# A transformer trunk on one core: the modulation steps moved off the keys and doubled in the later MLP, and the merge ordered by branches

## The chip, the cores and the metric

The kernel runs on one core of a Trainium2 chip. The metric is the device time of one execution in microseconds. Three runs of the kernel before gave 1308.4, 1308.9 and 1310.21, so its median is 1308.9 us.

## What is computed

The reference is a backbone of two layers over 512 tokens of 1024 channels, 256 of context and 256 latent ones on a grid. Cut to what matters:

```
for l in range(2):
    mod_lat = silu(c) @ w_ada[l] + b_ada[l]          # 6 x 1024: shift, scale, gate, twice
    mod_ctx = silu(c_ctx) @ w_ada[l] + b_ada[l]
    h = rms_norm(x) * (1 + sc1) + sh1                # context and latent, each with its own
    p = h @ w_in                                     # gate logits | c_q | c_kv | k_r | na q, k, v
    mq, mk, mv = from rms_norm(c_q) @ w_uq, rms_norm(c_kv) @ w_ukv, with rope
    y_mla = dense attention of 8 heads;  y_na = neighbourhood attention of 8 heads
    y = sigmoid(gates_a) * (y_mla @ w_mla_o) + sigmoid(gates_b) * (y_na @ w_na_o)
    x = x + gt1 * (y @ w_out)
    h2 = rms_norm(x) * (1 + sc2) + sh2
    x = x + gt2 * (relu(h2 @ w_ff1)**2 @ w_ff2)
```

In the last layer the context's queries, merge and MLP are left out, since only the latent stream is returned.

## The kernel before

Channels lie on the partitions and tokens along the free dimension. Every large product is made of three fp32r matmuls (`mm3`, L101 to L103): weights and data are split into a high and a low part, and high by high, high by low and low by high are added in PSUM. A weight tile of 128x1024 goes this way: SP issues its load into a ring of five raw buffers (`wraw`, L118), ScalarE writes the high part (`wsplit`, L129, `whi`), VectorE writes what is left (L130, `wlo`). There are three pairs of `whi` and `wlo`. The raw ring is shared by all weights and by the rows of the modulation, and SP issues all of them in the order of the program.

`proj_a` (L134) walks over output tiles in chunks of 128 channels. A chunk is 24 matmuls; after it come the evacuation, and one call of `step()` (L150).

`step` (L171) advances the side work, a generator that `ada_side` (L235) makes: the modulation, a product of one or two vectors with `w_ada`, done on VectorE. One part is 1024 of the 6x1024 outputs. A step of a part loads one block of 128 rows of `w_ada` (512 KB) and multiplies and adds it for each vector z (L250 for the first block, L254 afterwards). A step with both vectors is called one of two columns here, a step with one vector one of one column. Behind eight such steps come, per vector, a step that transposes and reduces in VectorE (L265, L266), and one that adds over the partitions on PE (L272) and writes `modT` (L276). The pieces are issued behind the last `wlo` of the moment (`issue_after(lead())`).

Three sides matter. The first makes the gate of the attention of layer 0: eleven steps of two columns, with four accumulators of 512 columns. Before, four of them are taken in the evacuation of the keys (`evac` of `w_ukv`, L743 and L744), and six in the chunks of the gates. What is left is done at `step(99)` behind the gates. The last side is made in the MLP of layer 0: seven parts of what layer 0's MLP and layer 1 need, the first three of two columns (33 steps), the last four of one column (40 steps). Before, each chunk of the MLP takes one step, each ff2 block but the last is closed by `step(4)` (L1200), and two steps are left for the end of the layer.

The MLP is run as ff1(0), ff1(1), ff2(0), ff1(2), ff2(1), ff1(3), ff2(2), ff2(3), each of eight chunks; "third block" below means ff1(2), and "second ff2 block" ff2(1).

The merge (L1031 to L1056) walks over pairs of output tiles. A pair has a weight tile of each branch (a for MLA, b for the neighbourhood attention). Before, for each of its two chunks j both branches are multiplied, then VectorE forms (gate + 1) * product for both (L1048), POOL adds the two (L1052, `m`; VectorE in the last pair), ScalarE takes the high part (L1053, `h`) and POOL what is left (L1054).

The products of each engine's queue are laid out by the scheduler of the framework from this program; within a queue, an engine keeps that order.

Of the kernel before, what the change touches and what calls it, by code (L numbers as in the profile page):

```python
# [45 lines left out]
def trunk(ctx: ExitStack, tc, t):  # L46
# [76 lines left out]

    split = []

    def wsplit(src, k, n):
# [6 lines left out]
    def proj_a(w, k0, kc, f0, nf, moves, cols, evac, bank=None, hook=None):  # L133
# [4 lines left out]
        for f in range(0, nf, per):  # L138
            raw = wraw(w, k0, kc, (f0 + f) * 128, per * 128)
            h, lo = wsplit(raw, kc, per * 128)  # L140
            for j in range(per):
                fs = slice(j * 128, (j + 1) * 128)
                o = (ps(bank[(f + j) % len(bank)]) if bank else psx())[:, :N]
                for k in range(kc):
                    if hook:
                        hook(f + j, k)
                    mm3(o, h[:, k, fs], lo[:, k, fs], mh(k)[:, cols], ml(k)[:, cols], k == 0, k == kc - 1)
                evac(f + j, o)
                flush()
                step()  # L150

# [312 lines left out]
    for l in range(DEPTH):  # L464
# [267 lines left out]
        for hf in range(2):  # L732
            def evac(tk, o):
# [7 lines left out]
                if hf == 1 and tk % 2:  # L741
                    k_stat(tk - 1)
                if tk % 2:  # L743
                    step()  # L744

# [286 lines left out]
        for f in range(0, 8, 2):  # L1032
# [3 lines left out]
            wab = [wsplit(wraw(w_, 0, 4, f * 128, 256), 4, 256) for w_ in (wa, wb)]  # L1036
            for j in range(2):
                zs = [None, None]
                fs = slice(j * 128, (j + 1) * 128)
                g2 = g2f[:, :, j]  # L1040
                for b in (0, 1):
                    (h, lo), (yh, yl) = wab[b], ys[b]
                    o = psx()[:, :TQ]
                    for k in range(4):
                        mm3(o, h[:, k, fs], lo[:, k, fs], yh(k), yl(k), k == 0, k == 3)
                    zs[b] = o
                for b in range(2):
                    nc.vector.scalar_tensor_tensor(out=g2[:, b], in0=g2[:, b], scalar=1.0, in1=zs[b],  # L1048
                                                   op0=ALU.add, op1=ALU.mult)
                eng = nc.vector if f + j >= 6 else nc.gpsimd  # L1050
                m = sp.tile([128, TT], F32, tag="tmp", name="m", bufs=NTMP)
                eng.tensor_tensor(out=m[:, :TQ], in0=g2[:, 0], in1=g2[:, 1], op=ALU.add)  # L1052
                nc.scalar.activation(out=gh[:, f + j, :], in_=m[:, :TQ], func=AF.Copy)  # L1053
# [132 lines left out]
        def ff2(g, a):  # L1186
# [12 lines left out]
            proj_a(t["w_ff2"][l], g * 8, 8, 0, 8, (lambda k: a[0][:, k], lambda k: a[1][:, k]), loc, res_add(GT2))  # L1199
            step(4)  # L1200

# [51 lines left out]
        flush()  # L1253
        step(99)
        pre_ctx = po_ctx

# [54 lines left out]
```

## Time and profile before

| | |
|---|---|
| median of three runs | 1308.9 us |
| the profiled execution | 1308.73 us, span 1306.9 us |
| mean granted clock of PE | 0.994 |
| PE busy | 1272.0 us (97%) |
| VectorE (DVE) busy | 907.8 us (69%) |
| ScalarE (ACT) busy | 582.3 us (45%) |
| POOL busy | 262.3 us (20%) |
| moved by DMA | 208.01 MB, mean 159 GB/s |

The profile is one execution on the chip. A view called a timeline gives instructions with their start and duration, and in brackets how long the engine was idle before and what it then waited for. A window gives busy times of all engines in a stretch, with the clock that TensorE was granted (1.00 is the upper of its two levels, 2.4 GHz; 0.50 the lower, 1.2 GHz). Matmuls are pipelined, so a duration in a timeline is longer than the distance from one start to the next. Where times of one stretch are named, they are microseconds from the start of the span: the keys lie at 97 to 125, the gates at 125 to 158, the attention of layer 0 behind them to 379, its merge at 379 to 426, its MLP at 478 to 826, the start of layer 1 at 826, and the merge of layer 1 at 1063 to 1090.

### The profile page before, as it was taken

What the parts mean: (1) busy time and instruction counts of PE and PEld (TensorE: products, weight loads), DVE (VectorE), ACT (ScalarE), POOL (GpSimd) and SP (SyncE); (2) the same over time, 40 slices, a digit from 0 to 9 for tenths busy, and PEclk for the clock granted to TensorE, in tenths of its full rate; (3) what the DMA queues carried; (4) which work ended last, traced back from release to release, by engine and by line L of the source; (5) the groups of instructions that cost most, each with busy time, mean ns of one, the idle gap of its engine ahead of it and who ended that gap; (6) DMA issues with size and microseconds to landing.
All of it is one profiled execution on the core that took longest, in us unless ns stands there. A gap on an engine that the chain in (4) does not pass through costs nothing.

```text
span 1306.9 us, 20364 instructions
## 1 busy us (share of the span) xinstructions
PE 1272.0 (97%) x7831; PEld 1093.3 (84%) x7831; DVE 907.8 (69%) x1547; ACT 582.3 (45%) x1054; POOL 262.3 (20%) x258
## 2 busy tenths in 40 slices
PE   7998999999999999999999999899999999999997
PEld 5697888986787898888888888899889779999896
DVE  4559687688985579899675675766763967665553
ACT  4455277445523344422322312366664645554452
POOL 0317402411004003210201200019132111121011
PEclk9998999999999999999999999899999999999999
DMA  9855600364486326566566574387214657646652
GB/s 292 291 110 161 209 29 22 100 193 64 110 308 202 99 64 197 163 204 200 167 197 209 170 226 141 115 172 213 74 44 119 129 179 206 169 160 192 193 186 89
DMA packets 241857, 208.01 MB, mean 159 GB/s; under 512 B 24464, under 2 KB 220816, under 8 KB 241376
## 3 DMA queue, kind: packets, MB, share of 16 engines
q1 hardware_dynamic: 231728, 190.16, 50.6%
q10 hardware_dynamic: 9520, 16.29, 3.5%
q8 instruction: 61, 1.00, 0.3%
q0 software_dynamic: 512, 0.27, 0.1%
q14 instruction: 36, 0.29, 0.1%
HBM read 195.15 MB, written 11.53 MB: 158 GB/s over the span
## 4 chain that ended last, share of the span: by engine, by line
PE 55%; DVE 2%; POOL 2%; issue 2%; ACT 1%; DMA 0%; POOLq 0%; ACTq 0%; DVEq 0%
PE psB L101 7%; PE psB L103 7%; PE psB L102 7%; PE psA L101 6%; PE psA L103 6%; PE psA L102 6%; PE psC L103 4%; PE psC L101 4%; PE psC L102 4%; DVE wlo L130 1%; PE psC L872 1%; PE psD L892 1%; ACT whi L129 1%; PE psB L926 1%; PE psD L101 0%
## 5 line engine op out<-in xcount | busy, mean ns | idle before, releaser
L130 DVE TENSOR_TENSOR wlo<-raw,whi 128x1024 fp32r<-128x1024 f32 (+3 forms) x252 | 310.6, 1234 | 189.8 <-ACT whi L129 188.6
L129 ACT ACTIVATE whi<-raw 128x1024 fp32r<-128x1024 f32 (+3 forms) x252 | 260.5, 1035 | 351.3 <-PE psB L102 116.7
L254 DVE SCALAR_TENSOR_TENSOR ada<-raw,silu,ada 128x1024 f32<-128x1024 f32 (+1 forms) x126 | 156.3, 1272 | 0.2
L102 PE MATMUL psA<-wlo,h 128*128 128x256 f32 (+2 forms) x408 | 120.9, 296 | 2.4 <-DVE wlo L130 2.4
L101 PE MATMUL psA<-whi,h 128*128 128x256 f32 (+2 forms) x408 | 121.0, 297 | 1.1 <-ACT h L344 1.1
L103 PE MATMUL psA<-whi,h 128*128 128x256 f32 (+2 forms) x408 | 120.8, 296 | 0.0
L101 PE MATMUL psB<-h,whi 128*128 128x256 f32 (+1 forms) x272 | 91.8, 338 | 0.1
L102 PE MATMUL psB<-h,whi 128*128 128x256 f32 (+1 forms) x272 | 91.8, 338 | 0.0
L103 PE MATMUL psB<-h,wlo 128*128 128x256 f32 (+1 forms) x272 | 91.6, 337 | 0.0
L101 PE MATMUL psA<-h,whi 128*128 128x512 f32 (+1 forms) x248 | 87.6, 354 | 1.1 <-ACT h L344 1.0
L102 PE MATMUL psA<-h,whi 128*128 128x512 f32 (+1 forms) x248 | 87.3, 352 | 0.2 <-DVE h L346 0.2
L103 PE MATMUL psA<-h,wlo 128*128 128x512 f32 (+1 forms) x248 | 87.1, 351 | 0.0
L102 PEld LDWEIGHTS psA<-wlo,h 128*128 128x128 f32 x408 | 78.3, 192 | 4.7 <-DVE wlo L130 2.6
L101 PEld LDWEIGHTS psA<-whi,h 128*128 128x128 f32 x408 | 78.3, 192 | 3.3 <-ACT h L344 1.6
L103 PEld LDWEIGHTS psA<-whi,h 128*128 128x128 f32 x408 | 78.3, 192 | 2.3 <-issue 0.4
L1165 POOL TENSOR_TENSOR h<-s,h 128x512 fp32r<-128x512 f32 (+1 forms) x32 | 38.0, 1190 | 168.5 <-ACT h L1164 151.1
L1165 POOL TENSOR_TENSOR fl<-s,fa 128x512 fp32r<-128x512 f32 (+1 forms) x32 | 35.3, 1104 | 164.8 <-ACT fa L1164 164.8
L101 PE MATMUL psB<-G,whi 128*128 128x512 f32 (+2 forms) x192 | 66.8, 348 | 0.0
L103 PE MATMUL psB<-G,wlo 128*128 128x512 f32 (+2 forms) x192 | 66.3, 345 | 0.3 <-DVE wlo L130 0.3
L102 PE MATMUL psB<-G,whi 128*128 128x512 f32 (+2 forms) x192 | 66.5, 346 | 0.0
L101 PE MATMUL psC<-G,whi 128*128 128x258 f32 (+2 forms) x200 | 62.6, 313 | 0.0
L103 PE MATMUL psC<-G,wlo 128*128 128x258 f32 (+2 forms) x200 | 62.5, 312 | 0.0
(388 smaller groups left out, 3333.0 us busy)
## 6 DMA issues: line engine op xcount, KB each, us to landing
raw<-in_w_ff_dram SPq DMA_DIRECT2D x128, 512.0 KB, 4.3
raw<-in_w_ada_dram SPq DMA_DIRECT2D x80, 512.0 KB, 3.7
raw<-in_w_in_dram SPq DMA_DIRECT2D x62, 512.0 KB, 4.6
raw<-in_w_out_dram SPq DMA_DIRECT2D x16, 512.0 KB, 4.6
spare<-in_w_ada_dram SPq DMA_DIRECT2D x12, 512.0 KB, 8.9
xT_d<-xT SPq DMA_DIRECT2D x2, 2048.0 KB, 13.1
bias<-in_rpb_dram SPq DMA_DIRECT2D x64, 64.0 KB, 7.1
g_d<-g ACTq DMA_DIRECT2D x16, 256.0 KB, 3.9
```

Of the source, the lines that this page charges most:

```text
L101: nc.tensor.matmul(out, sh, mh, start=first, stop=False)
L102: nc.tensor.matmul(out, sh, ml, start=False, stop=False)
L103: nc.tensor.matmul(out, sl, mh, start=False, stop=last)
L129: nc.scalar.activation(out=hi, in_=src, func=AF.Copy)
L130: split[:] = [nc.vector.tensor_tensor(out=lo, in0=src, in1=hi.bitcast(F32), op=ALU.subtract).ins]
L254: nc.vector.scalar_tensor_tensor(out=a, in0=raw[:, c:c + w], scalar=sc, in1=a, op0=ALU.mult, op1=ALU.add)
L872: nc.tensor.transpose(o[:, kt * 256 + i * 128:kt * 256 + (i + 1) * 128], pt[:, (kp * 2 + kt) * 128:(kp * 2 + kt + 1) * 128], perm if K == ...
L892: mm = nc.tensor.matmul(yo[z * 64:(z + 1) * 64, oc], vsel(kt, 2 * hp + z), tr[kt // 2][:, kt % 2, :], start=kt == nkt - 1, stop=kt == 0, t ...
L926: mm = nc.tensor.matmul(os[z], q_[zs, cs], k_[zs, :K], start=n == 0, stop=n == 2)
L1165: nc.gpsimd.tensor_tensor(out=al[:, f, :], in0=s[:, :TQ], in1=ah[:, f, :].bitcast(F32), op=ALU.subtract)
```

## The change

Four edits. No step is taken in the keys any more; the gates still take six, so five are left to `step(99)` behind them. `step(4)` at the end of an ff2 block is replaced by a pace: `proj_a` takes `pace[0]` steps after each chunk, which is 1 until the end of ff2(0) and 2 from there. With two a chunk the side's 73 steps end in ff2(2), none is left for ff2(3) or the layer's end. The merge runs both chunks of branch a, then both of branch b, and forms each (gate + 1) * product right behind its product; the additions, `h` and the rest come behind all four.

```
--- before.py
+++ after.py
@@ -122,6 +122,7 @@
         return raw
 
     split = []
+    pace = [1]
 
     def wsplit(src, k, n):
         hi, lo = hl_tile()
@@ -147,7 +148,7 @@
                     mm3(o, h[:, k, fs], lo[:, k, fs], mh(k)[:, cols], ml(k)[:, cols], k == 0, k == kc - 1)
                 evac(f + j, o)
                 flush()
-                step()
+                step(pace[0])
 
     def proj_tail(w, k0, fs, moves, halves, evac, hook):
 
@@ -740,8 +741,6 @@
                 head_ss(krr[:, tk, hs], dst, 4, NOPE, rs)
                 if hf == 1 and tk % 2:
                     k_stat(tk - 1)
-                if tk % 2:
-                    step()
 
             proj_b(loader(t["w_ukv"][l], 0, hf * 512, 512, 2, 1), 1, lambda k: ch[:, 6 + k], lambda k: cl[:, 6 + k],
                    [0, 1, 2, 3], 512, evac)
@@ -1034,22 +1033,21 @@
                 nc.scalar.dma_start(out=xT, in_=xT_d[:, :, c_q])
             g2f = g2s[f // 2]
             wab = [wsplit(wraw(w_, 0, 4, f * 128, 256), 4, 256) for w_ in (wa, wb)]
-            for j in range(2):
-                zs = [None, None]
-                fs = slice(j * 128, (j + 1) * 128)
-                g2 = g2f[:, :, j]
-                for b in (0, 1):
-                    (h, lo), (yh, yl) = wab[b], ys[b]
+            zs = {}
+            for b in (0, 1):
+                (h, lo), (yh, yl) = wab[b], ys[b]
+                for j in range(2):
+                    fs = slice(j * 128, (j + 1) * 128)
                     o = psx()[:, :TQ]
                     for k in range(4):
                         mm3(o, h[:, k, fs], lo[:, k, fs], yh(k), yl(k), k == 0, k == 3)
-                    zs[b] = o
-                for b in range(2):
-                    nc.vector.scalar_tensor_tensor(out=g2[:, b], in0=g2[:, b], scalar=1.0, in1=zs[b],
+                    zs[b, j] = o
+                    nc.vector.scalar_tensor_tensor(out=g2f[:, b, j], in0=g2f[:, b, j], scalar=1.0, in1=o,
                                                    op0=ALU.add, op1=ALU.mult)
+            for j in range(2):
                 eng = nc.vector if f + j >= 6 else nc.gpsimd
                 m = sp.tile([128, TT], F32, tag="tmp", name="m", bufs=NTMP)
-                eng.tensor_tensor(out=m[:, :TQ], in0=g2[:, 0], in1=g2[:, 1], op=ALU.add)
+                eng.tensor_tensor(out=m[:, :TQ], in0=g2f[:, 0, j], in1=g2f[:, 1, j], op=ALU.add)
                 nc.scalar.activation(out=gh[:, f + j, :], in_=m[:, :TQ], func=AF.Copy)
                 eng.tensor_tensor(out=gl[:, f + j, :], in0=m[:, :TQ], in1=gh[:, f + j, :].bitcast(F32),
                                   op=ALU.subtract)
@@ -1197,7 +1195,7 @@
                 nxt.extend((*nh, acc, norm_1))
                 return
             proj_a(t["w_ff2"][l], g * 8, 8, 0, 8, (lambda k: a[0][:, k], lambda k: a[1][:, k]), loc, res_add(GT2))
-            step(4)
+            pace[0] = 2
 
         if last:
 
@@ -1252,6 +1250,7 @@
         second(3, prev)
         flush()
         step(99)
+        pace[0] = 1
         pre_ctx = po_ctx
 
     po_ctx.close()
```

Line numbers of the kernel after differ by one or two from those before (L250 is L251, L1163 is L1161).

On VectorE in the keys, ahead of the first copy of a key product (L738 before, L739 after), there stood

```order
L250 TENSOR_SCALAR ada<-raw,silu 128x512 x4
L254 SCALAR_TENSOR_TENSOR ada<-raw,silu,ada 128x512 x4
L605 TENSOR_REDUCE qrs<-sq 128x2 x2
L130 TENSOR_TENSOR wlo<-raw,whi 128x1024
L254 SCALAR_TENSOR_TENSOR ada<-raw,silu,ada 128x512 x6
L605 TENSOR_REDUCE qrs<-sq 128x2
L254 SCALAR_TENSOR_TENSOR ada<-raw,silu,ada 128x512 x2
L605 TENSOR_REDUCE qrs<-sq 128x2
L130 TENSOR_TENSOR wlo<-raw,whi 128x1024
L738 COPY mqk<-psB 128x4x64 x2
```

and now there stands

```order
L131 TENSOR_TENSOR wlo<-raw,whi 128x1024
L606 TENSOR_REDUCE qrs<-sq 128x3
L606 TENSOR_REDUCE qrs<-sq 128x2 x2
L131 TENSOR_TENSOR wlo<-raw,whi 128x1024
L606 TENSOR_REDUCE qrs<-sq 128x2
L131 TENSOR_TENSOR wlo<-raw,whi 128x1024
L606 TENSOR_REDUCE qrs<-sq 128x2
L739 COPY mqk<-psB 128x4x64 x2
L251 TENSOR_SCALAR ada<-raw,silu 128x512 x2
```

The sixteen pieces of the modulation ahead of the copy are gone; the first L251 comes behind it. (`qrs` are the sums of squares of the queries.)

On VectorE at the end of the third ff1 block there stood (`s` is the square of the rectified product, L1163 before and L1161 after)

```order
L1163 TENSOR_TENSOR s<-r 128x512
L265 STREAM_TRANSPOSE ada<-ada 128x512 x2
L266 TENSOR_REDUCE red<-ada 128x16 x2
L250 TENSOR_SCALAR ada<-raw,silu 128x1024
L130 TENSOR_TENSOR wlo<-raw,whi 128x1024
L1163 TENSOR_TENSOR s<-r 128x512
L265 STREAM_TRANSPOSE ada<-ada 128x512 x2
L266 TENSOR_REDUCE red<-ada 128x16 x2
L254 SCALAR_TENSOR_TENSOR ada<-raw,silu,ada 128x1024
L276 TENSOR_TENSOR modT_99<-psC,pT 32x16 x4
L130 TENSOR_TENSOR wlo<-raw,whi 128x1024
L1163 TENSOR_TENSOR s<-r 128x512
```

and now

```order
L131 TENSOR_TENSOR wlo<-raw,whi 128x1024
L1161 TENSOR_TENSOR s<-r 128x512
L266 STREAM_TRANSPOSE ada<-ada 128x512 x2
L267 TENSOR_REDUCE red<-ada 128x16 x2
L266 STREAM_TRANSPOSE ada<-ada 128x512 x2
L267 TENSOR_REDUCE red<-ada 128x16 x2
L1161 TENSOR_TENSOR s<-r 128x512
L277 TENSOR_TENSOR modT_99<-psC,pT 32x16 x4
L251 TENSOR_SCALAR ada<-raw,silu 128x1024
L255 SCALAR_TENSOR_TENSOR ada<-raw,silu,ada 128x1024 x4
L1161 TENSOR_TENSOR s<-r 128x512
L131 TENSOR_TENSOR wlo<-raw,whi 128x1024
```

Between the last `wlo` of the third block and the first of the second ff2 block there are now both columns' transposes and reduces, `modT`, and five pieces of the next part. On SP, the loads from the third block's last ones on were, before,

```order
L118 DMA raw<-in_w_ff_dram 128x8x128 x4
L118 DMA raw<-in_w_ada_dram 128x1024
L118 DMA raw<-in_w_ff_dram 128x8x128
L118 DMA raw<-in_w_ada_dram 128x1024
L118 DMA raw<-in_w_ff_dram 128x8x128
```

and are

```order
L118 DMA raw<-in_w_ff_dram 128x8x128 x2
L118 DMA raw<-in_w_ada_dram 128x1024
L118 DMA raw<-in_w_ff_dram 128x8x128
L118 DMA raw<-in_w_ada_dram 128x1024 x2
L118 DMA raw<-in_w_ff_dram 128x8x128
L118 DMA raw<-in_w_ada_dram 128x1024 x2
L118 DMA raw<-in_w_ff_dram 128x8x128
```

Two rows of the modulation stand between two weights, where one did. The last row is the first weight of the second ff2 block.

On VectorE at the boundary of the layers (`h` is the normed input of layer 1, the `wlo` of 576 columns the third weight tile of its first product) there stood

```order
L340 SCALAR_TENSOR_TENSOR u<-xT,A_1_101,psD 128x256
L346 SCALAR_TENSOR_TENSOR h<-u,modT_99,h 128x256
L265 STREAM_TRANSPOSE ada<-ada 128x512
L346 SCALAR_TENSOR_TENSOR h<-u,modT_99,h 128x256
L266 TENSOR_REDUCE red<-ada 128x16
L265 STREAM_TRANSPOSE ada<-ada 128x512
L130 TENSOR_TENSOR wlo<-raw,whi 128x576
L266 TENSOR_REDUCE red<-ada 128x16
L276 TENSOR_TENSOR modT_99<-psC,pT 32x8 x4
L322 TENSOR_SCALAR ms<-psC 128x2
```

and now

```order
L347 SCALAR_TENSOR_TENSOR h<-u,modT_99,h 128x256
L341 SCALAR_TENSOR_TENSOR u<-xT,A_1_101,psD 128x256
L347 SCALAR_TENSOR_TENSOR h<-u,modT_99,h 128x256
L131 TENSOR_TENSOR wlo<-raw,whi 128x576
L347 SCALAR_TENSOR_TENSOR h<-u,modT_99,h 128x256
L323 TENSOR_SCALAR ms<-psC 128x2
L341 SCALAR_TENSOR_TENSOR u<-xT,A_1_101,psC 128x256 x3
```

The two transposes, two reduces and `modT` are gone from between `h` and the first weights and the sum of squares.

## Rows read from the trace of the kernel before

**Rows 1.** The page's first part, of the whole span: busy time, share of the span and instructions of each engine.
```profile
PE 1272.0 (97%) x7831; PEld 1093.3 (84%) x7831; DVE 907.8 (69%) x1547; ACT 582.3 (45%) x1054; POOL 262.3 (20%) x258
```

**Rows 2.** The waits of PE over the whole span: the product that waited (its PSUM bank and line), what it waited for, us in total, how often, and the longest in us.
```profile
PE psB L101 <- ACT mv L739: 4.9, 1, 4.9
PE psA L102 <- DVE wlo L130: 2.4, 1, 2.4
PE psA L101 <- ACT h L344: 2.1, 3, 1.1
PE psC L103 <- DVE wlo L130: 1.7, 2, 1.5
PE psC L330 <- POOL rt L179: 1.0, 2, 0.6
```

**Rows 3.** The timeline of DVE in the keys: start in us, duration in us, engine, line, operation, tiles, count, and in brackets the idle time before it with its releaser. Lines that are not needed are left out.
```profile
102.05 1.67 DVE L250 TENSOR_SCALAR ada<-raw,silu 128x512 f32<-128x512 f32 x4
103.63 3.71 DVE L254 SCALAR_TENSOR_TENSOR ada<-raw,silu,ada 128x512 f32<-128x512 f32 x4
...
108.91 4.06 DVE L254 SCALAR_TENSOR_TENSOR ada<-raw,silu,ada 128x512 f32<-128x512 f32 x6
...
113.15 2.26 DVE L254 SCALAR_TENSOR_TENSOR ada<-raw,silu,ada 128x512 f32<-128x512 f32 x2
...
116.74 0.74 DVE L738 COPY mqk<-psB 128x256 f32<-128x256 f32 x2
```

**Rows 4.** The timeline of PE in the keys, with the same columns.
```profile
117.77 0.79 PE L101 MATMUL psB<-whi,G 128*128 128x512 f32 x1 [4.93 <-ACT mv L739]
```

**Rows 5.** Windows in the keys: the stretch, its length, busy us (instructions) of PE, PEld, DVE, ACT and POOL, the granted clock of PE, the DMA engines' share and GB/s.
```profile
114.00:116.00 2.00, 0.00 (x0) 0.00 (x0) 2.00 (x4) 0.00 (x0) 1.92 (x3) 0.95 0.31 119
116.00:122.00 6.00, 4.23 (x10) 3.36 (x11) 6.00 (x11) 4.21 (x9) 5.76 (x7) 0.50 0.62 179
122.00:125.00 3.00, 3.00 (x13) 2.36 (x13) 3.00 (x7) 1.63 (x4) 2.92 (x3) 0.89 0.00 0
```

**Rows 6.** A window over the head pair of the MLA branch of layer 0 that has 37 filler products, with the same columns.
```profile
195.50:213.40 17.90, 17.37 (x127) 14.17 (x126) 14.23 (x41) 12.16 (x29) 6.00 (x6) 1.00 0.05 19
```

**Rows 7.** Windows over the merge of layer 0 and the merge of layer 1, with the same columns.
```profile
379.00:426.00 47.00, 44.99 (x196) 36.18 (x195) 28.60 (x39) 12.96 (x16) 16.60 (x12) 1.00 0.69 241
1063.00:1090.00 27.00, 23.94 (x184) 22.13 (x184) 16.04 (x27) 10.12 (x16) 12.11 (x12) 1.00 0.81 242
```

**Rows 8.** The timeline of DVE in the merge of layer 0.
```profile
397.11 0.69 DVE L1048 SCALAR_TENSOR_TENSOR g<-g,psA 128x512 f32<-128x512 f32 x1 [1.88 <-PE psA L103]
```

**Rows 9.** The timeline of POOL in the merge of layer 0.
```profile
392.80 1.30 POOL L1052 TENSOR_TENSOR m<-g 128x512 f32<-128x512 f32 x1 [1.20 <-ACT h L1053]
```

**Rows 10.** The page's costliest groups of instructions: line, engine, operation, tiles, count, then busy us, mean ns of one, and idle time before with its releaser.
```profile
L130 DVE TENSOR_TENSOR wlo<-raw,whi 128x1024 fp32r<-128x1024 f32 (+3 forms) x252 | 310.6, 1234 | 189.8 <-ACT whi L129 188.6
L129 ACT ACTIVATE whi<-raw 128x1024 fp32r<-128x1024 f32 (+3 forms) x252 | 260.5, 1035 | 351.3 <-PE psB L102 116.7
L254 DVE SCALAR_TENSOR_TENSOR ada<-raw,silu,ada 128x1024 f32<-128x1024 f32 (+1 forms) x126 | 156.3, 1272 | 0.2
```

**Rows 11.** The page's DMA issues: tile and source, queue, count, KB each, median us from issue to landing.
```profile
raw<-in_w_ff_dram SPq DMA_DIRECT2D x128, 512.0 KB, 4.3
```

**Rows 12.** The timeline of ACT in the MLP of layer 0, late in the first ff2 block and at the start of the third ff1 block.
```profile
597.29 1.06 ACT L129 ACTIVATE whi<-raw 128x1024 fp32r<-128x1024 f32 x1 [5.61 <-DMA raw<-in_w_ff_dram]
...
613.63 0.58 ACT L1161 ACTIVATE r<-psB 128x512 f32<-128x512 f32 x1
```

**Rows 13.** The timeline of DVE at the end of the third ff1 block.
```profile
636.70 0.68 DVE L1163 TENSOR_TENSOR s<-r 128x512 f32<-128x512 f32 x1
637.30 1.30 DVE L265 STREAM_TRANSPOSE ada<-ada 128x512 f32<-128x512 f32 x2
638.52 1.24 DVE L266 TENSOR_REDUCE red<-ada 128x16 f32<-128x512 f32 x2
```

**Rows 14.** The timeline of DVE at the boundary of the layers.
```profile
833.93 0.71 DVE L265 STREAM_TRANSPOSE ada<-ada 128x512 f32<-128x512 f32 x1
...
836.14 0.72 DVE L130 TENSOR_TENSOR wlo<-raw,whi 128x576 fp32r<-128x576 f32 x1
...
838.02 0.69 DVE L276 TENSOR_TENSOR modT<-psC,pT 32x8 f32<-32x8 f32 x4 [0.56 <-PE psC L272]
```

**Rows 15.** Windows in the MLP and at the start of the next layer, with the columns of the windows above.
```profile
580.00:600.00 20.00, 20.00 (x90) 16.57 (x89) 17.76 (x27) 4.04 (x4) 0.00 (x0) 1.00 0.54 171
...
830.00:834.00 4.00, 4.00 (x33) 4.00 (x32) 4.00 (x11) 2.29 (x6) 0.00 (x0) 1.00 0.76 307
```

**Rows 16.** The timeline of PE at the start of the third ff1 block of layer 0.
```profile
607.12 0.47 PE L101 MATMUL psB<-G,whi 128*128 128x512 f32 x1
```

**Rows 17.** The timeline of PE at the boundary of the layers.
```profile
836.92 0.40 PE L102 MATMUL psA<-wlo,h 128*128 128x288 f32 x1 [2.37 <-DVE wlo L130]
...
842.07 0.61 PE L101 MATMUL psA<-whi,h 128*128 128x288 f32 x1 [1.11 <-ACT h L344]
```

**Rows 18.** Windows at the boundary of the layers, with the same columns.
```profile
834.00:838.00 4.00, 1.63 (x14) 1.40 (x12) 3.46 (x7) 0.17 (x1) 0.00 (x0) 1.00 0.94 297
838.00:842.00 4.00, 2.40 (x13) 1.87 (x12) 1.81 (x8) 0.49 (x2) 0.70 (x1) 0.68 0.68 182
842.00:846.00 4.00, 3.93 (x16) 3.93 (x17) 4.00 (x11) 1.73 (x5) 0.00 (x0) 0.50 0.00 0
```

More of the change, by code (lines that the diff above doesn't have):

```diff
@@ L124, in trunk @@
     split = []
+    pace = [1]
     def wsplit(src, k, n):
@@ L149, in proj_a @@
                 flush()
-                step()
+                step(pace[0])
     def proj_tail(w, k0, fs, moves, halves, evac, hook):
@@ L742, in evac @@
                     k_stat(tk - 1)
-                if tk % 2:
-                    step()
             proj_b(loader(t["w_ukv"][l], 0, hf * 512, 512, 2, 1), 1, lambda k: ch[:, 6 + k], lambda k: cl[:, 6 + k],
@@ L1036, in trunk @@
             wab = [wsplit(wraw(w_, 0, 4, f * 128, 256), 4, 256) for w_ in (wa, wb)]
[L1037 to L1042, printed above, removed]
+            zs = {}
+            for b in (0, 1):
+                (h, lo), (yh, yl) = wab[b], ys[b]
+                for j in range(2):
+                    fs = slice(j * 128, (j + 1) * 128)
                     o = psx()[:, :TQ]
@@ L1045, in trunk @@
                         mm3(o, h[:, k, fs], lo[:, k, fs], yh(k), yl(k), k == 0, k == 3)
-                    zs[b] = o
-                for b in range(2):
-                    nc.vector.scalar_tensor_tensor(out=g2[:, b], in0=g2[:, b], scalar=1.0, in1=zs[b],
+                    zs[b, j] = o
+                    nc.vector.scalar_tensor_tensor(out=g2f[:, b, j], in0=g2f[:, b, j], scalar=1.0, in1=o,
                                                    op0=ALU.add, op1=ALU.mult)
+            for j in range(2):
                 eng = nc.vector if f + j >= 6 else nc.gpsimd
                 m = sp.tile([128, TT], F32, tag="tmp", name="m", bufs=NTMP)
-                eng.tensor_tensor(out=m[:, :TQ], in0=g2[:, 0], in1=g2[:, 1], op=ALU.add)
+                eng.tensor_tensor(out=m[:, :TQ], in0=g2f[:, 0, j], in1=g2f[:, 1, j], op=ALU.add)
                 nc.scalar.activation(out=gh[:, f + j, :], in_=m[:, :TQ], func=AF.Copy)
@@ L1199, in ff2 @@
             proj_a(t["w_ff2"][l], g * 8, 8, 0, 8, (lambda k: a[0][:, k], lambda k: a[1][:, k]), loc, res_add(GT2))
-            step(4)
+            pace[0] = 2
         if last:
@@ L1254, in trunk @@
         step(99)
+        pace[0] = 1
         pre_ctx = po_ctx
```

## The prediction, made before the change was run

> **What bounds the kernel.** I read the shares of the page first, then the list of TensorE's waits, then timelines and windows around the waits that the edits touch. PE is busy for 97% of the span [rows 1], so only what PE waits for, and stretches with its clock halved, can move the end. In the list of waits [rows 2] the reader is to see that the longest, 4.9 us, is in the keys, that the next, 2.4 us, is at the boundary of the two layers, and that the rest are short. The MLP hardly appears there: its products follow each other without a gap. The profiled execution took 1308.73 us, 0.2 under the median of the runs shown; the sums are made against it. A change within 0.2% (2.6 us) can't be told from no change.
>
> **Keys.** VectorE works from 102.05 through sixteen one-column pieces of the modulation (L250, L254) with little between them, and so comes to the copy of the first key product, L738, at 116.74 only [rows 3]. Behind the copy is ACT's `mv`, and PE stands for 4.93 us for the PSUM bank that `mv` frees [rows 4]. By the order of VectorE above none of the sixteen stands ahead of that copy now. They are 1.67+3.71+4.06+2.26 = 11.7 us, over twice the wait, so I take it as gone: −4.9. The clock is at half from 116 to 122, where ten matmuls of 512 columns took 4.23 us; the next three us hold 13, 0.23 each [rows 5], so ten cost 2.0 too much. Without the wait nothing halves the clock: −2.0. Together **−6.9**. The moved pieces go beside the gates, where a chunk is 24 such matmuls, 5.5 us, against 1.2 of `wlo` and four pieces of 0.7 to 1.1 on VectorE: covered, and without that cover each step would cost PE 2.7 or more. Bounds: −3, if the next thing in line holds the bank for over half the time, and −7.5.
>
> **Attention of layer 0.** The earlier keys shift PE's order here: 37 filler products (256 columns, an estimated 0.115 us each, half of 0.23) that stood in the second head pair of the MLA branch come in elsewhere. A pair with 37 of them takes 17.9 us, PE 17.4 of it and VectorE 14.2 [rows 6]. Such a pair without 37 has 13.1 us of PE, while two more `wlo` bring VectorE to 16.6. The fillers are worked off elsewhere at no loss, so the loss is at most the hole, 0 to 4.3; I take rather under half, **+1.8**, since the pairs before ran with nearly no gap.
>
> **Merge of layer 0.** PE idles 2.0 of 47 us in it [rows 7], most of it in one wait for `wlo`, 1.5 [rows 2]. That goes, since the weights of the next pair stand ahead of `h` now. But the next `whi` but one stands behind an `h` on ACT that waits for the product of the second branch: a piece of 0.7 on VectorE [rows 8], POOL's addition 1.3 [rows 9], `h` 0.5 (an estimate, half of a `whi`), `whi` 1.0 and `wlo` 1.2 [rows 10], together 4.7, less the one chunk of 2.7 (12 matmuls of 0.23) and two matmuls that PE has left: +1.5. **−0.5**, between −2 and +1.
>
> **Merge of layer 1.** PE idles 3.1 us in it [rows 7]. `whi` still stands behind `h` on ACT, and `h` comes later in a pair than before. **+0.5**, between −3 (all gone) and +3 (doubled).
>
> **MLP of layer 0.** The queue of weights decides here. The raw ring has five buffers for weights and modulation rows together, SP issues in order, and a load starts when the load five places ahead of it has been used. It takes 4.3 us to land [rows 11], and before the change one already made ACT wait for data at 597.29 [rows 12]. At two steps a chunk the ring holds under two chunks.
> In the third block (two columns a step) a chunk costs VectorE 1.2 of `wlo`, 0.7 of `s` and 4×1.27 [rows 10, 13], 7.0 us, against 5.5 of PE: 1.5 too much for five chunks, 7.5, against two chunks ahead, 10.9. No wait yet.
> At the end of that block, by the order above, transposes and reduces of two columns, `modT`, one L251 and four L255 stand between two `wlo`. I walk it in the clock of before. The transposes and reduces of one column take 2.4 from 637.30 [rows 13]; two columns end at 642.1. `s` 0.7, `modT` 0.7 and L251 0.7 follow (`modT` by its like at the boundary [rows 14], L251 at half an L254 and a little): 644.2, and a buffer for the next modulation load is free. One L255 later, at 645.5, so is the one for the next block's weight; two modulation loads stand ahead of it in SP's order, at 1.7 us each (0.524 MB at 307 GB/s [rows 15]). It lands at 644.2+4.3+3.4 = 651.9. Behind it come `whi` 1.1 and `r` 0.6 on ACT [rows 12], `s` 0.7 and `wlo` 1.2: 655.5. PE begins the block at 607.12 [rows 16], ends eight chunks of 5.45 at 650.8 and needs `wlo` in the third matmul, at 651.3: a wait of 4.2. If loads don't share their rate, it is 0.8. I take **+3.3**, nearer to the walk; the range is 0 to 5.
>
> **Layer boundary.** Before, the last of the modulation stands between the next layer's norm and its first weights: VectorE transposes from 833.93, and `wlo` of the third weight starts at 836.14 [rows 14]. PE waits 2.37 for it [rows 17]. PE is in order, so the sum of squares, POOL's root (L330) and `h` come late too: 0.6 and 1.1 more [rows 2, 17]. Then the clock falls (0.68 over 838 to 842, so at half from 839.4) and 16 matmuls take 3.93 us, twice their time [rows 18]: 1.9, and some 0.3 before 842. Now no modulation is left there and `wlo` follows the pieces of `h` directly (order above). 2.4+0.6+1.1+1.9+0.3 = 6.3; the chain through POOL's root stays, so **−6.2**, between −3 and −7.
>
> Sum: −6.9+1.8−0.5+0.5+3.3−6.2 = **−8.0**: 1300.7 in the profiled execution's terms, 1300.9 beside the median.
>
> **Rivals.**
> (1) Transfers keep up, and the MLP shows no wait: 1300.9−3.3 = 1297.6. For it: three loads of 0.524 MB in 5.45 us are 289 GB/s, and 307 have been moved [rows 15]. Against: a `whi` waited for its load in a stretch that moved 171 [rows 12, 15], so the buffers bind before the rate does. The Trainium skill ("Perfetto Trace Analysis", section Roofline) lets a core that streams alone go up to about 435 GB/s; by that rule nothing would wait here, and no run here shows such a rate. 0.22.
> (2) The wait in the MLP, or the hole in the attention, halves the clock. In the keys the clock fell some 3 us after PE stopped (0.95 over 114 to 116 [rows 5]), so 3.3 us is at the edge; the stop of 2.37 alone left it at 1.00 [rows 17, 18]. The price is ten to sixteen matmuls at half speed, 2.0 to 3.4: 1304. The Trainium skill ("TensorE: Matmul & The Clock Gate", section Part 1: The HAM clock gate) calls the slow clock the default, which only activity lifts; by it a long stop is paid twice, as the keys show. 0.12.
> (3) One of the two gains doesn't come, since another chain (POOL's root at the boundary, ACT in the keys) stands right behind: 5 less, 1306. Against: VectorE's backlog was more than twice the wait. 0.10.
> (4) Slower: the knot at the third block's end recurs in each of the four one-column parts, 4×3.3 more: 1314.1. It decides if under 4 us of weights are ahead whenever a `modT` comes. Against: those parts have half the columns. 0.05.
>
> **How the numbers follow.** The forecast has 0.51. Faster by over 0.2% (under 1306.3) are the forecast, (1), (2) and half of (3), which lies at the limit: 0.90. The other half of (3) gives 0.05 within 0.2%, (4) gives 0.05 slower. The range goes from 1296.0, which is (1) with no hole in the attention, to (3)'s 1306.0; (4) and the tails of the terms are left out.
>
> **What would show it.** In the profile after: no wait for `mv` and no half clock near 113 to 122; none of the modulation near the boundary, and no half clock there; one wait for `wlo` at the start of the second ff2 block, some 640 us into the run, with ACT's `whi` waiting for a load. I am wrong if the MLP waits in several places, or if PE still waits for the keys' bank.

## The result, and the profile after

The changed kernel took 1302.61 us in the median of four runs (1301.52 to 1304.18), the kernel before 1309.56 beside it: a ratio of 0.9948 [0.993, 0.9965]. A second set gave 0.9948 [0.9935, 0.9962]. The prediction was 1300.9, in a range of 1296 to 1306. The profiled execution took 1301.52 us, 1.1 under that median; its span is 1299.7.

The page's first part, to set beside [rows 1]:

```profile
PE 1267.2 (97%) x7831; PEld 1090.3 (84%) x7831; DVE 914.2 (70%) x1547; ACT 582.4 (45%) x1054; POOL 264.2 (20%) x258
```

As many instructions run on every engine as before; the difference is in when. The waits of PE over the whole span (PSUM bank and line, what was waited for, us in total, how often, the longest):

```profile
PE psD L383 <- DMA crow<-in_c_ctx_dram: 3.7, 1, 3.7
PE psA L431 <- DMA xrow<-in_ctx_dram: 3.5, 2, 1.9
PE psA L103 <- DVE wlo L131: 3.2, 3, 1.2
PE psA L101 <- ACT mv L740: 1.6, 1, 1.6
PE psA L101 <- ACT h L345: 1.5, 3, 0.8
PE psA L101 <- ACT whi L130: 1.4, 1, 1.4
PE psC L871 <- DVE qk L774: 1.3, 1, 1.3
PE psD L891 <- DVE ri L840: 1.3, 1, 1.3
PE psC L101 <- ACT whi L130: 1.0, 1, 1.0
PE psC L103 <- DVE wlo L131: 1.0, 1, 1.0
```

Beside [rows 2], the 4.9 us for `mv` and the 2.4 for `wlo` at the boundary are gone, and these are new or grown: `psA L103` (1.18 us in the MLP, 0.89 and 1.18 in the merge of layer 1), `mv` in another place, `qk`, `ri` and three for `whi` and `wlo` in the merges. The two waits for a DMA stand in the first 9 us of the program. The kernel before has them too, with 3.5 and 3.3 us; [rows 2] leaves them out, so the 2.4 at the boundary was not the second longest in its list. A list of waits says neither where they are nor what a halved clock adds, so I set PE's timelines against each other: the start of each product after, less its start before. Every profile has a shift at 97 us already (from -1.1 to +1.9 us; the three that are late by 1.6 or more have a half clock at 21 us); it is taken off. All figures are worked out so, in us; the second column is another profile of the changed kernel.

| stretch (in us of before) | predicted | change | again |
|---|---|---|---|
| keys, to the first gate at 125 | -6.9 | -7.5 | -7.5 |
| attention of layer 0, to 360 | +1.8 | +2.7 | +2.1 |
| end of the attention and merge of layer 0, to 429 | -0.5 | -0.1 | -0.1 |
| MLP, to 826 | +3.3 | +2.0 | +2.4 |
| boundary, to 858 | -6.2 | -6.0 | -6.0 |
| keys of layer 1, 882 to 900 | 0 | +1.9 | +1.7 |
| the rest, with the merge of layer 1 | +0.5 | +0.1 | 0 |
| sum | -8.0 | -7.0 | -7.4 |

**Keys.** Windows over the stretch of [rows 5] (length, busy us and instructions of PE, PEld, DVE, ACT, POOL, granted clock, DMA share, GB/s):

```profile
112.00:114.00 2.00, 2.00 (x11) 1.65 (x10) 2.00 (x6) 1.68 (x4) 1.92 (x4) 1.00 0.27 107
114.00:116.00 2.00, 2.00 (x10) 1.69 (x9) 2.00 (x4) 1.00 (x3) 2.00 (x2) 1.00 0.32 81
116.00:122.00 6.00, 6.00 (x28) 4.95 (x27) 6.00 (x11) 3.72 (x9) 5.83 (x5) 1.00 0.49 150
```

PE is busy all the time, and the stretch that had ten matmuls at half clock has 28 at 1.00. The gates behind it take 32.64 us as before, though VectorE has only 0.2 us of pause in them.

**MLP.** Timelines of ACT, DVE, SP and PE at the start of the second ff2 block (start, duration, engine, line, operation, tiles, count, and in brackets the idle time before it with its releaser):

```profile
644.23 1.06 ACT L130 ACTIVATE whi<-raw 128x1024 fp32r<-128x1024 f32 x1 [6.15 <-DMA raw<-in_w_ff_dram]
```
```profile
624.81 1.43 DVE L131 TENSOR_TENSOR wlo<-raw,whi 128x1024 fp32r<-128x1024 f32 x1 [1.69 <-ACT whi L130]
...
630.25 1.23 DVE L131 TENSOR_TENSOR wlo<-raw,whi 128x1024 fp32r<-128x1024 f32 x1 [3.40 <-ACT whi L130]
...
638.20 1.80 DVE L251 TENSOR_SCALAR ada<-raw,silu 128x1024 f32<-128x1024 f32 x1
640.04 5.25 DVE L255 SCALAR_TENSOR_TENSOR ada<-raw,silu,ada 128x1024 f32<-128x1024 f32 x4
...
646.42 1.22 DVE L131 TENSOR_TENSOR wlo<-raw,whi 128x1024 fp32r<-128x1024 f32 x1
```
```profile
626.27 5.56 SPq L118 DMA_DIRECT2D raw<-in_w_ada_dram  x2
640.04 0.38 SPq L118 DMA_DIRECT2D raw<-in_w_ff_dram  x1
641.36 1.65 SPq L118 DMA_DIRECT2D raw<-in_w_ada_dram  x2
```
```profile
647.69 0.50 PE L103 MATMUL psA<-fa,wlo 128*128 128x512 f32 x1 [1.18 <-DVE wlo L131]
```

This is the forecast wait, in the forecast matmul: the third of the block waits for a `wlo` whose `whi` waited for its load. It is 1.2 us and not 3.3, because the load went out at 640.04, as soon as L251 had freed a buffer. The two modulation loads that stand ahead of it in SP's order had gone out long before: at 626.27 and 631.50, each right behind the end of a `wlo` of the third block (626.24 and 631.48). My walk had them still to come at that point. Some 0.5 more is lost around 659 and 0.3 later.

**Boundary.** Windows for those of [rows 18], whose clock was 0.68 and 0.50:

```profile
834.00:838.00 4.00, 3.56 (x27) 3.32 (x26) 4.00 (x12) 2.81 (x6) 0.00 (x0) 1.00 0.97 258
838.00:842.00 4.00, 3.90 (x29) 3.50 (x27) 3.79 (x9) 3.56 (x10) 0.00 (x0) 1.00 0.17 14
842.00:846.00 4.00, 3.96 (x33) 4.00 (x34) 3.83 (x8) 3.22 (x12) 0.00 (x0) 1.00 0.55 39
```

Eighty-nine instructions of PE where there were 43 in the same twelve us, and the clock at 1.00 throughout. No piece of the modulation is left there.

**Keys of layer 1**, which the prediction left out. Timelines of PE, ACT and SP:

```profile
881.34 0.50 PE L101 MATMUL psA<-whi,G 128*128 128x512 f32 x1 [1.61 <-ACT mv L740]
```
```profile
875.48 1.06 ACT L130 ACTIVATE whi<-raw 128x1024 fp32r<-128x1024 f32 x1 [2.95 <-DMA raw<-in_w_ukv_dram]
```
```profile
860.88 1.25 SPq L814 DMA_DIRECT2D bias<-in_rpb_dram  x2
862.23 0.55 SPq L118 DMA_DIRECT2D raw<-in_w_ukv_dram  x1
862.83 2.95 SPq L814 DMA_DIRECT2D bias<-in_rpb_dram  x2
865.88 0.68 SPq L118 DMA_DIRECT2D raw<-in_w_ukv_dram  x1
```

The second load of the key and value weights goes out 7.6 us earlier than before (865.88 for 873.50), while PE comes 9.2 us earlier: part of the boundary's gain is handed back as a late load.

### The profile page after: what moved, and what is told of

Its sections match the earlier page's. It is cut to its first block, busy times and chain, and to the rows that moved or that the text cites. A ratio compares the mean times of both kernels' runs of the same rounds, so it can differ in the third digit from the quotient of the medians.

```text
span 1299.7 us, 20369 instructions
## 1 busy us (share of the span) xinstructions
PE 1267.2 (97%) x7831; PEld 1090.3 (84%) x7831; DVE 914.2 (70%) x1547; ACT 582.4 (45%) x1054; POOL 264.2 (20%) x258
## 4 chain that ended last, share of the span: by engine, by line
PE 52%; DVE 4%; DMA 3%; issue 2%; POOL 2%; ACT 2%; SPq 0%; POOLq 0%; ACTq 0%; DVEq 0%
PE psB L101 6%; PE psB L102 6%; PE psB L103 6%; PE psA L103 6%; PE psA L101 6%; PE psA L102 6%; PE psC L103 4%; PE psC L101 4%; PE psC L102 4%; DVE wlo L131 2%; ACT whi L130 1%; PE psD L891 1%; DMA raw<-in_w_na_o_dram 1%; PE psC L871 1%; DMA raw<-in_w_ukv_dram 1%
## 5 line engine op out<-in xcount | busy, mean ns | idle before, releaser
L255 DVE SCALAR_TENSOR_TENSOR ada<-raw,silu,ada 128x1024 f32<-128x1024 f32 (+1 forms) x126 | 160.7, 1310 | 0.5
L103 PE MATMUL psA<-whi,h 128*128 128x256 f32 (+2 forms) x408 | 120.3, 295 | 0.0
L103 PE MATMUL psB<-h,wlo 128*128 128x256 f32 (+1 forms) x272 | 91.6, 337 | 0.0
L103 PE MATMUL psA<-h,wlo 128*128 128x512 f32 (+1 forms) x248 | 87.1, 351 | 0.0
L103 PEld LDWEIGHTS psA<-whi,h 128*128 128x128 f32 x408 | 77.8, 191 | 1.9
L1163 POOL TENSOR_TENSOR h<-s,h 128x512 fp32r<-128x512 f32 (+1 forms) x32 | 38.7, 1210 | 170.7 <-ACT h L1162 153.4
L1163 POOL TENSOR_TENSOR fl<-s,fa 128x512 fp32r<-128x512 f32 (+1 forms) x32 | 35.1, 1098 | 163.9 <-ACT fa L1162 163.9
L103 PE MATMUL psB<-G,wlo 128*128 128x512 f32 (+2 forms) x192 | 66.2, 345 | 0.3 <-DVE wlo L131 0.3
L103 PE MATMUL psC<-G,wlo 128*128 128x258 f32 (+2 forms) x200 | 62.5, 312 | 0.0
```

The lines of the kernel that those rows point to most:

```text
L103: nc.tensor.matmul(out, sl, mh, start=False, stop=last)
L255: nc.vector.scalar_tensor_tensor(out=a, in0=raw[:, c:c + w], scalar=sc, in1=a, op0=ALU.mult, op1=ALU.add)
L1163: nc.gpsimd.tensor_tensor(out=al[:, f, :], in0=s[:, :TQ], in1=ah[:, f, :].bitcast(F32), op=ALU.subtract)
```

## The experiments

My theory: the five terms above are the whole story, each bound to one edit. Rivals: the losses belong to other edits or to noise; and, for each loss, another cause (VectorE or bandwidth, not order). Ratios are to the kernel before, on the same chip.

**The keys' edit alone.**

```
-                if tk % 2:
-                    step()
```

> The kernel before with the edit of the keys alone. In the profile of the changed kernel the gates began 7.8 us earlier than before, and 2.6 us of that were lost in the attention of layer 0, mostly in waits for VectorE (1.33 us at 173.52, 1.27 us at 317.63); in layer 1's keys 1.8 us more were lost. Theory A: the two losses have different causes. The attention's comes with the keys' edit, because the steps not taken in the keys leave the second pair of heads with 3 gate products between its transposes where it had 9; the loss in layer 1's keys comes from the boundary, so it is absent here. Then the gates begin 7.7 to 7.9 us earlier, the attention gives back 2.2 to 3.0, the MLP and layer 1 move by less than 0.5, and the time is 4.5 to 5.5 us below that of before: a ratio of 0.9958 to 0.9966. Theory B: the loss in the attention is noise of one profile or comes from somewhere else; then the gain of the keys arrives whole, 7 to 8 us, a ratio of about 0.9943. The prediction's own terms (6.9 less 1.8) give 5.1 us, 0.9961.

Measured: 1302.35 us, 0.9955 [0.9943, 0.9967]. The ratio goes with the means, which lie 5.9 us apart; the medians lie 7.1 apart. By the time alone, Theory B is at the edge of the interval, so the profile decides. In it the gates begin 7.5 us earlier, the attention gives back 1.9, and the merge gains 0.6, which was not expected. Theory A holds for the attention, whose loss comes with this edit. For layer 1's keys it holds in the main: they wait 0.35 us for `mv` and give back 0.6, where the changed kernel waits 1.61 and gives back 1.9.

**The pace alone** (L150, L1200 and the reset; the keys and the merge as before).

```
-                step()
+                step(pace[0])
-            step(4)
+            pace[0] = 2
```

> The kernel before with the pace edit alone (two steps a chunk from the third block of layer 0's MLP on, none left for its end). Theory A: the boundary between the layers gains 6 to 6.5 us, the MLP loses 1.5 to 2.5 with a wait of PE for the low part of the second ff2 block's first weights (about 1.2 us), and the start of layer 1 gives back 1.5 to 2.1 in its keys, where PE waits for a value low part that is late because the weights of the value half land late. Together 2 to 3 us below before, a ratio of 0.9977 to 0.9985. Theory B: what was lost in layer 1's keys belongs to another part of the change (or to the earlier start of everything); then no wait in layer 1's keys, and 4 to 4.7 us below before, 0.9964 to 0.9970. The prediction's own terms (6.2 less 3.3) give 2.9 us, 0.9978.

Measured: 1306.91 us (twelve runs, 1304.29 to 1310.26), 0.9981 [0.9972, 0.9989], 2.5 us below: Theory A. The boundary gains 6.0 and the MLP loses 2.3. Layer 1's keys give back 3.7, with the same wait for `mv`, 1.85 us. The profiled run is the slowest of the twelve, and its stretches add up to a gain of only 0.1, so its give-back is no median. PE's timeline shows the wait, and the second of two windows the lowered clock that came behind it:

```profile
887.98 0.70 PE L101 MATMUL psA<-whi,G 128*128 128x512 f32 x1 [1.85 <-ACT mv L740]
```
```profile
880.00:886.00 6.00, 6.00 (x30) 4.83 (x29) 2.52 (x4) 3.24 (x6) 2.37 (x3) 1.00 1.02 283
886.00:892.00 6.00, 4.15 (x12) 3.19 (x12) 4.16 (x11) 4.21 (x9) 5.84 (x8) 0.72 0.82 220
```

**The merge alone** (the loop over branches of the diff, nothing else).

```
-            for j in range(2):
-                for b in (0, 1):
+            for b in (0, 1):
+                for j in range(2):
```

> The kernel before with the merge edit alone. Theory A, from the two profiles: PE waits as long in each merge as before, only at other products (layer 0: 2.0 us of waits for the high and low part of weights for 2.1 before; layer 1: 3.5 for about 3.2), so the time is within 1 us of before, a ratio of 0.9992 to 1.0008. Theory B: the edit gains 1 to 2 us by itself, and the changed kernel hides it, since its merges start earlier against their weight loads; 0.9985 to 0.9992. Theory C: it loses 1 to 2 us, 1.0008 to 1.0015, and the changed kernel would be faster without it.

Measured: 1309.41 us for 1309.41, 1.0001 [0.9993, 1.001]: Theory A, nothing. In its list of waits the one of 1.5 us in layer 0's merge is replaced by two of 1.0, as in the changed kernel:

```profile
PE psC L101 <- ACT whi L129: 1.0, 1, 1.0
...
PE psC L103 <- DVE wlo L130: 1.0, 1, 1.0
```

In the merge of layer 1 the edit costs 0.4 us, by this profile and by both of the changed kernel. The short waits of before, of at most 0.76 us, are gathered into long ones, among them 1.44 us for `whi` and 0.89 for `wlo` right behind it, and a lowered clock follows them (0.58 over the next four us). Windows of the changed kernel:

```profile
1060.00:1064.00 4.00, 1.67 (x13) 1.27 (x11) 2.01 (x2) 2.57 (x4) 2.87 (x4) 1.00 0.42 145
1064.00:1068.00 4.00, 4.00 (x21) 4.00 (x22) 1.75 (x2) 1.22 (x2) 0.43 (x1) 0.58 0.88 275
```

By their ratios the three edits alone make 5.9, 2.5 and -0.1 us, together 8.3; the changed kernel gains 6.9. The intervals are wide enough to take up the difference, and I draw nothing from it.

**The pace one block later.**

```
+            if g == 1:
+                pace[0] = 2
             proj_a(t["w_ff2"][l], ...
-            pace[0] = 2
```

> The changed kernel, but the pace of two starts one block later, at the second ff2 block, so that the third block takes one step a chunk; the 73 steps still end inside ff2(2). Theory A (the ring of raw buffers): what made PE wait at 647.69 were modulation loads ahead of the weight load that the second ff2 block needed, eight more of them in the third block than before. With one step a chunk there, that wait of 1.18 us goes, and with it about 0.5 hidden ones around 659; the parts of one column behind it are crossed at two steps a chunk, as in the changed kernel, where VectorE never starved. 1.2 to 2 us below the changed kernel, a ratio to before of 0.9932 to 0.9939, no wait of over 0.3 us at the start of the second ff2 block. Theory B: the wait only moves: the same number of steps is pressed into fewer chunks, and PE waits as long at ff1(3) or ff2(2) when they come to two a chunk; then no difference from the changed kernel, 0.9948. The boundary stays at its 22.2 us under both.

Measured: 1300.99 us, 0.9939 [0.9927, 0.9951]. This interval and that of the changed kernel overlap, so it is the profile that shows Theory A: no wait of PE of over 0.2 us is left between 600 and 720, and the whole MLP costs 0.2 us where it cost 2.0. The window of 20 us from 640, of the changed kernel and of this one:

```profile
640.00:660.00 20.00, 18.80 (x81) 14.72 (x80) 19.20 (x20) 6.36 (x8) 3.75 (x2) 1.00 0.81 262
```
```profile
640.00:660.00 20.00, 20.00 (x90) 16.36 (x89) 13.70 (x24) 5.41 (x7) 3.59 (x3) 1.00 0.38 117
```

From 660 to 680 both move 290 to 300 GB/s with PE at 20.00: the one-column parts at two steps a chunk cost nothing, and rival (4) of the prediction has no ground.

**The bias rows of layer 1 on ScalarE's queue.**

```
-                    nc.sync.dma_start(out=bias[...], in_=src)
+                    (nc.scalar if l else nc.sync).dma_start(out=bias[...], in_=src)
```

> The changed kernel, with layer 1's sixteen loads of the attention's bias rows (64 KB each) issued on ScalarE's DMA queue instead of SP's. In both profiles SP needs 27 us from the first of them to the second load of the key and value weights (838.90 to 865.88 after, 846.36 to 873.50 before) and is issuing all through it; behind the change PE comes to layer 1's keys 9.2 us earlier, SP only 7.6. Theory A (order on SP): that load is late because it stands behind twelve bias loads of 1.2 to 3 us each on SP. Without them it is issued some 20 us earlier, ScalarE's high part no longer waits 2.95 us for it, PE's wait of 1.61 us for the value copy at 881.34 goes, and the time is 1.3 to 2.3 us below the changed kernel: a ratio to before of 0.9930 to 0.9938. Theory B (transfers): the bias rows take the DMA engines' time wherever they are issued, the weights land as late, and nothing changes: 0.9948. Theory C: ScalarE, which evacuates the queries in that stretch, is held up by the issues, and PE waits for it: 1 us or more above the changed kernel.

The edit moves 32 loads, not sixteen: those named, and sixteen more at 1009 to 1030, in layer 1's attention. Also, of the sixteen named only five held SP for 1.9 to 3.0 us; the other eleven held it for 0.6.

Measured: 1300.99 us, 0.9939 [0.9926, 0.9952], again with an interval that overlaps the changed kernel's. Theory A in place, and in size by the medians: the wait for `mv` is gone, and the stretch from 882 to 900 gives nothing back (0.0 for 1.9). One number in it was wrong: the load is issued 2.7 us earlier against PE, not 20 (SP's timeline; the second of the two goes out at 865.39). What holds it next I take to be the ring of raw buffers; no run tests that.

```profile
862.26 3.50 SPq L118 DMA_DIRECT2D raw<-in_w_ukv_dram  x2
```

The Trainium skill ("DMA: Bandwidth & Descriptors", section Rules for kernel authors) says that spreading loads over issuing engines saves only their issue time; this run fits that, and the time saved was worth 1.6 us by the medians. Its profile gains 1.2 us more between 900 and 1130. There the three waits in layer 1's merge (1.44, 0.89 and 1.18) and its lowered clock are gone, while the attention before it has three new ones (0.82, 0.72 and 1.66) and another order of filler products. Which of the moved loads does which stays open, and the medians don't show the 1.2.

**All of the first side's steps in the gates.**

```
             for _ in range(n):
                 f = ngate[0]
+                if l == 0:
+                    pace[0] = 1 + (f >= 1)
...
         step(99)
+        pace[0] = 1
```

> The changed kernel, but all eleven steps are taken in the gates (two a chunk from the second chunk on), none is left for behind them. The scheduler then puts as many gate products between the transposes of the second pair of heads as in the kernel before (9; the changed kernel has 3 there, 34 in the gap behind for 33, 48 in the one ahead for 28). Theory A (fillers): the attention's loss of 2.6 us comes from that order; PE's waits at 173.52 and 174.93 (1.33 and 0.51 us) go, and the time is 1.5 to 2.6 us below the changed kernel, a ratio to before of 0.9928 to 0.9937, if VectorE, already busy for 33 of the 33 us from 117 to 150, gets through the gates in time. Theory B (VectorE): the four more steps, some 1.4 us each per block of four, come ahead of the low parts of the gates' weights, and PE waits for them in the gates by more than 2 us: no faster than the changed kernel, 0.9948 or above. Theory C: the loss in the attention has nothing to do with the fillers: the waits at 173 to 175 stay and the time is that of the changed kernel.

The edit did more than it says: `gates` is called once more behind the attention, and there it set the pace to two again, for the merge and the whole MLP. So the total, 1338.47 us, 1.023 [1.0215, 1.0244], says nothing of the gates; the stretch up to 280 us does. There both A and B came true. With the gate products placed as before, the attention loses nothing (PE's shift is -3.0 at the end of the gates and at 280), and no wait is left at 173. But the gates now take 37.1 us for 32.64, with a stop of 2.59 us for `wlo` (PE's timeline) and a lowered clock around it (a window):

```profile
141.31 0.50 PE L103 MATMUL psB<-h,wlo 128*128 128x512 f32 x1 [2.59 <-DVE wlo L131]
```
```profile
138.00:146.00 8.00, 5.41 (x18) 3.95 (x17) 8.00 (x10) 2.43 (x3) 7.75 (x7) 0.79 0.80 216
```

More is lost there, 4.5 us, than the attention gives. (The expectation counts four more steps in the gates; it is five.)

**A control: nine of eleven steps in the gates**, the same edit with `f >= 3`.

> A control for the kernel with all steps in the gates: two steps a chunk only from the fourth gate on, so nine of eleven are taken there and two are left. The order of the gate products between the heads' transposes is that of the changed kernel (48, then 11, 34, 3), only VectorE's work stands earlier. Theory A (fillers): the waits in the second pair of heads stay, 1.3 and 0.5 us, and the time is within 0.7 us of the changed kernel. Theory B (VectorE is late at the first heads because it is still at the modulation): the waits shrink with the work that is left, and the time is 1 us or more below the changed kernel.

Up to 280 us it is Theory A. The waits stay, at the same products and in the same size, though less of VectorE's work is left; the attention loses 2.3 us, as in the changed kernel over that stretch:

```profile
174.19 0.66 PE L874 MATMUL psC<-ident,P 128*128 128x128 f32 x4 [1.35 <-DVE qk L777]
175.60 0.66 PE L874 MATMUL psC<-ident,P 128*128 128x128 f32 x4 [0.51 <-ACT PT L878]
```

What counts is the three gate products in that gap for nine. The flaw of the other kernel is here too (1337.48 us), and the two together price it: at two steps a chunk from the MLP's start, the parts of two columns lose 28.5 and 29.6 us by the end of the third block, in waits for `wlo` of up to 5.4 us. That the changed kernel doubles the pace only later is not a detail.

**A ring of four.** `NRAW` 4 for 5.

> The changed kernel with four raw buffers instead of five for every weight. Theory A (the ring): the wait at the start of the second ff2 block is there because a load can only be issued when a buffer of the ring is free, and modulation rows hold buffers until VectorE has used them; with one buffer fewer, PE's waits in the MLP from 600 to 720 grow from 1.2 us to 3 us or more, and in layer 1's keys, where the load waits for SP, nothing changes. Theory B (bandwidth): the transfers themselves set it, at 262 to 300 GB/s from 640 to 700; then the waits there stay within 0.5 us of the changed kernel's. The whole time is expected 3 to 15 us above the changed kernel under A, less than 2 under B.

Measured: 1309.7 us, 1.0005 [0.9993, 1.0016], 7 us above the changed kernel. In the MLP 5.7 us are lost between 560 and 660 for 1.5; the load for the second ff2 block goes out 3.2 us later (SP's and PE's timelines below), while less is moved (238 GB/s from 640 to 660, 262 in the changed kernel). That is the ring. Another 6.0 us are lost in the queries of layer 1, in a wait of 3.26 us at 869.61 with a half clock behind it, which the expectation did not have. Behind that the keys give back nothing, where the changed kernel gives back 1.9; that nothing would change there was wrong.

```profile
643.24 0.38 SPq L118 DMA_DIRECT2D raw<-in_w_ff_dram  x1
```
```profile
649.15 0.50 PE L101 MATMUL psA<-fa,whi 128*128 128x512 f32 x1 [1.42 <-ACT whi L130]
```

**Late pace and bias rows together**, and the changed kernel again beside it.

> The changed kernel with both improvements: the pace of two from the second ff2 block on, and layer 1's bias rows on ScalarE's queue. Each alone gave a ratio of 0.9939 to before, for 0.9948 of the changed kernel. Theory A: they act at different places (the MLP at 640 to 660, layer 1's keys at 881) and their gains of 1.6 us add: 1299.4 us, a ratio of 0.9923 to 0.9932; no wait over 0.3 us at the start of the second ff2 block and none for the value copy in layer 1's keys. Theory B: what one gains, a transfer behind it takes back (the MLP ends earlier against layer 1's loads, which start no earlier), and the two together are worth one: 0.9939.

> The changed kernel once more, on the same chip as the kernel with both improvements, since it had four runs so far. All theories: a ratio of 0.9948 to before, within 0.0012; the waits at 647.69 (low part of weights, 1.2 us) and 881.34 (value copy, 1.6 us) are there again.

Measured: 1298.33 us, 0.9917 [0.9903, 0.9931], and the changed kernel 1302.29, 0.9948 [0.9935, 0.9962]. The gains add (Theory A), with neither wait left, and here the two intervals lie apart. This version beats both kernels.

## Why the prediction was right

**Keys** (-6.9, measured -7.5): right in mechanism and place, -7.5 being the bound I gave. Nothing stood next in line, and the gates covered the moved pieces. The two kernels with more in the gates show how thin that cover is: three more steps there cost 0.6 us, five 4.5.

**Attention** (+1.8, measured 2.1 and 2.7; 1.9 for the edit alone): the hole is where I put it, and the loss comes from missing gate products. The loss was taken too small. The hole is smaller than 37 products: from the pair's first transposes to the next pair's, 27 filler products stand where 58 stood, so 31 went, some 3.6 us; but 2.3 of that is lost by 280, well over the "rather under half" of the prediction. Three of its waits stand in that pair (173.52, 174.93 and 179.57 us), and they recur in every kernel with this order. A fourth, 1.27 us at 317.63, is 0.55 in the second profile and accounts for most of the difference between the two.

**Merges** (0 together, measured 0): in layer 0 the wait for `wlo` went, as said, and two of 1.0 us came in its place, one of them for the `whi` behind `h`. The -0.5 for layer 0 was not there (-0.1). The +0.5 for layer 1 was there (+0.4), with a lowered clock that the prediction did not have; the table's last line hides it, since other stretches gain 0.3 to 0.4.

**MLP** (+3.3, measured 2.0 and 2.4): mechanism, block and matmul right, size too large. The step that was mis-sized is the walk's "two modulation loads stand ahead of it in SP's order, at 1.7 us each": they do, but both had been issued by 631.50. The walk has them wait because of its rule that "a load starts when the load five places ahead of it has been used". By that rule the first of them waits for L251, and the weight for the first L255. In the run a load took the buffer that came free first: the two took those of weights that had just been split, and the weight took L251's. So the weight landed for ACT 4.2 us after its issue, with no 3.4 on top. The walk's other value, 0.8, is nearer to the 1.18; L251 took 1.80 for 0.74, which puts 1.1 on it, and a shorter chain and a later PE take 0.7 off. The walk's other half held: it has PE need `wlo` at 651.3 in the clock of before, 646.0 in this profile (PE is 5.3 us earlier), and 647.69 less 1.18 is 646.51.

**Boundary** (-6.2, measured -6.0): right.

**What failed** is a sentence that is not there: layer 1 was taken to follow the boundary unchanged. Its transfers did not. SP's issues from the first bias row to the second load of these weights, 27 us, moved up by 7.6 us and PE by 9.2, and 1.9 were handed back. The trace of before had the hint: at 882.78 the `whi` of those weights had waited 1.01 us for its load already.

**The sum** is nearer than its terms, and that is partly luck: the MLP's 1.3 too much and the keys' 0.6 too little make up for the 1.9 that is missing in layer 1.

**The rivals.** (1), no wait in the MLP, did not come: a stretch of 262 GB/s had the wait and one of 300 had none, so the ring's order decided, not the rate; the late pace makes it true. The Trainium skill ("Perfetto Trace Analysis", section Roofline) lets a streaming core go on to about 435 GB/s. The prediction's "no run here shows such a rate" is wrong: the kernel before itself moved 419 over eight us of its first merge, by this window.

```profile
384.00:392.00 8.00, 8.00 (x35) 6.47 (x35) 5.98 (x14) 0.37 (x1) 1.28 (x1) 1.00 1.02 419
```

(2), a halved clock, did not come at the two places that it names: the stops of 1.18 us in the MLP and 1.33 in the attention show a clock of 1.00. Its measure of 3.3 us "at the edge" did not hold, though: the clock fell behind shorter stops: in the merge of layer 1 in the changed kernel itself (0.58, behind 1.44 and 0.89 us), in the keys of layer 1 in the kernel with the pace alone (0.72, around 1.85), and in the MLP with a ring of four (0.79 over 648 to 656, with 1.42 and 0.53). (3) and (4) did not come.

## What to carry to other kernels

When a stall on the main engine goes, follow what it was a cushion for: list the transfers behind that place, see how early each can be issued, and subtract the gain from that margin. A side job that fits beside one kind of chunk does not fit beside all; move its pace block by block, with the busy time of the helping engine in that block. And test each edit alone: of these, two made all of the gain and nearly all of the losses, and one nothing in sum.

## What the runs showed of the chip

- Stops of like length cost differently by what follows. One of 1.61 us in the changed kernel cost 1.9 in all, with the clock at 1.00; one of 1.85 in the kernel with the pace alone cost 3.7, with 0.72 over the six us around it; one of 2.59 in the gates 4.5, with 0.79; the 4.93 of before 7.5, with 0.50. Even the same stops differ: two of 1.0 us in the merge of layer 0 left the clock at 1.00 in the changed kernel (first window) and had 0.69 around the second in the kernel with both improvements (second window).

```profile
398.00:402.00 4.00, 2.98 (x14) 2.13 (x13) 1.73 (x1) 2.64 (x3) 4.00 (x3) 1.00 0.58 171
```
```profile
398.00:402.00 4.00, 3.00 (x10) 2.04 (x9) 1.64 (x1) 2.64 (x3) 4.00 (x3) 0.69 0.59 180
```

- Of the sixteen loads of 64 KB of bias rows at the start of layer 1, the longest held SP for 3.0 us, at a median of 0.61; on ScalarE's queue the longest took 1.03, and the median landing was 6.1 us for 7.9. Of the sixteen later ones one took 2.47 us on ScalarE's queue, for 1.73 on SP. The same bytes moved; what differs is the queue that issued them and what was issued beside them.
